# Twelve transposes that nobody reads, beside the chunk scan of a state space layer

## The chip, the cores and the metric

The program runs on one core of a Trainium2 chip. TensorE multiplies matrices and writes PSUM banks; VectorE and ScalarE do elementwise work and empty PSUM; GpSimd does a little elementwise work; DMA queues, most of them issued from SyncE, bring inputs and weights. Each engine works through its own queue in order and waits on semaphores where it needs another engine's result. The metric is the device time of one execution in microseconds (us).

## What is computed

The reference is a trunk of two layers on 512 tokens with 1024 channels. Layer 0 mixes tokens with a diagonal complex state space model, layer 1 with sparse attention (an indexer picks 128 keys for each query); a SwiGLU block follows each. The change concerns layer 0's mixer only:

```python
a_bar = jnp.exp(lam * dt)
b_bar = ((a_bar - 1.0) / lam)[..., None] * lax.complex(b_re, b_im)
bu = jnp.einsum('blgh,gph->blgp', ug, b_bar)              # 64 groups of 16 channels, 64 states each
_, states = lax.associative_scan(_ssm_combine, (a_seq, bu), axis=1)
y = jnp.einsum('blgp,ghp->blgh', states, c).real.reshape(bsz, length, D_MODEL)
y = jax.nn.gelu(y + d_skip * u)
val, gate = jnp.split(y @ w_glu, 2, axis=-1)
return val * jax.nn.sigmoid(gate)
```

## The kernel before

**Tiling.** The 512 tokens are cut into 64 chunks of 8 tokens. The 64 groups are worked in 8 units (u = 0 to 7) of 8 groups. For a unit, `tables(u)` (VectorE) makes the weights W that carry a chunk's tokens into its state; `turned` transposes them on TensorE into a bank of the PSUM tag "tr" and ScalarE copies them out; `chunk_inputs` (TensorE, L679) makes each chunk's contribution S4; `lags` (TensorE, L697, into a "tr" bank that `lags_out` empties on VectorE at L703 as Kd) makes the part within a chunk, which small DMAs spread into M (L706). `turns` and `turns_out` make rotation factors E and ES.

**The scan.** `scan(u)` makes the chunk states X on VectorE: it rotates S4 (L758 to L760, giving z1), runs two real scans over the chunks (L764, giving z), rotates back into a second z1 and z2 (L768, L769) and adds into X (L773). z1, z2 and z lie in scratch buffers 2, 3 and 4, X in 5 or 6. Each scratch buffer is single, so a new tile in it waits until every reader of the old one is done. Buffer 4 also holds the second k3 of `readout` (L791) for every unit but the first; the first k3 uses 5 or 6.

**Outputs.** `readout(u)` makes VV on VectorE (L790 to L792; one buffer). `outputs` (TensorE, L800 from M and L801 from X and VV) writes two accumulators, ScalarE's GELU (L806) makes yg, `out` transposes it (L814, a "tr" bank), and ScalarE and VectorE split it into a high and a low part y (L819, L820). Between these, `filler` puts blocks of the gated projection (three matmuls a step, L272 to L274), for the groups that are ready, into TensorE's queue; ScalarE moves their sums out as `part` (L862). After the eighth unit the rest of the gated projection follows, then the SwiGLU block.

**Order.** The code emits instructions in the order of the loop at L914: scan(u), turns and turned of u+1, tokens of u+2, chunk inputs of u+1, filler, outputs of u, lags of u+1, tables of u+2, readout of u+1, out of u. A planner then fixes each engine's queue before the run, from its own costs and from what is ready by them. Only VectorE and ScalarE, and only up to the end of u = 0, are held to the emitted order among the instructions of that region (L433 to L949). TensorE's queue is the planner's throughout. A tag of PSUM banks has a number of banks, and a new tile waits for one to come free:

```python
    def tr(self):
        return self.pp.tile([P, S], F32, name="tr", bufs=2)
```

Of the kernel before, what the change touches and what calls it, by code (L numbers as in the profile page):

```python
# [20 lines left out]
P = 128  # L21
# [184 lines left out]
class Trunk:  # L206
# [160 lines left out]
    def s5(self, gain_row, x_ap, lre, lim, ldt, b_re, b_im, c_re, c_im, d_ap, w_glu):  # L367
        nc, tc = self.nc, self.tc
        V, PL, AC, PE = nc.vector, nc.gpsimd, nc.scalar, nc.tensor
        ident = self.ident  # L370
# [371 lines left out]
        def turns_out(u, E):  # L742
# [4 lines left out]
            AC.activation(RT[:, u % 2, :, 1:], r8[:, gs].unsqueeze(2).to_broadcast([P, UGP, NCH - 1]), AF.Copy)  # L747
            return ES

        def scan(u, S4, E, ES, between=None):  # L750
            sh = [P, 2, UGP, NCH]
            X = self.scratch(5 + u % 2, [P, UGP, 2, NCH], "X")
            PL.memset(X[:, :, :, 0:1], 0.0)
            z1 = self.scratch(2, sh, "z1")
            z2 = self.scratch(3, sh, "z2")
            z = self.scratch(4, sh, "z")
            Eb = E[:, 0:1].to_broadcast(sh)
            V.tensor_tensor(z1, S4, Eb, op=ALU.mult)  # L758
            V.tensor_tensor(z2, S4[:, ::-1], ES, op=ALU.mult)
            V.tensor_tensor(z1, z1, z2, op=ALU.add)  # L760
            if between is not None:
                between()
            for i in range(2):
                V.tensor_tensor_scan(z[:, i].rearrange("p g c -> p (g c)"), RT[:, u % 2].rearrange("p g c -> p (g c)"),  # L764
                                     z1[:, i].rearrange("p g c -> p (g c)"), 0.0, ALU.mult, ALU.add)
            z1 = self.scratch(2, sh, "z1")
            z2 = self.scratch(3, sh, "z2")
            V.tensor_tensor(z1, z, Eb, op=ALU.mult)  # L768
            V.tensor_tensor(z2, z[:, ::-1], ES[:, ::-1], op=ALU.mult)  # L769
            for i in range(2):  # L770
                for g2 in range(2):
                    hs = slice(g2 * SP, (g2 + 1) * SP)
                    V.tensor_tensor(X[i * SP : (i + 1) * SP, :, g2, 1:], z1[hs, i, :, : NCH - 1],  # L773
                                    z2[hs, i, :, : NCH - 1], op=ALU.add)
            return X
# [52 lines left out]
        groups, n = [], 0  # L828
        while n < len(order):
# [4 lines left out]
            n = m  # L834
# [73 lines left out]
        tokens(1)  # L908
        spread(1)
        X0 = scan(0, S4[0], E[0], ES[0])  # L910
        VV = readout(0)
        W[1] = tables(1)
        normal(2)
        for u in range(UN):  # L914
            more = u + 1 < UN
            X = scan(u, S4[u], E[u], ES[u]) if u else X0
            f = PIECES[u]
            if more:
# [471 lines left out]
```

## Time and profile before

| | |
|---|---|
| time, median of 3 runs | 1292.81 us (1292.65 to 1295.38) |
| the profiled execution's own time | 1294.01 us |
| its span in the profile | 1292.3 us |
| TensorE (PE) busy | 1228.5 us, 95% |
| VectorE (DVE) busy | 769.0 us, 60% |
| ScalarE (ACT) busy | 543.3 us, 42% |
| mean granted TensorE clock | 0.991 |

The profile is of one execution. Times count from the span's start. PE is TensorE's matmuls (a transpose is one of them), PEld its weight loads, DVE is VectorE, ACT ScalarE, POOL GpSimd. A matmul's end is modelled, and consecutive matmuls overlap, so a run of them is shorter than the sum of its members.

### The profile page before, as it was taken

The page shows a single profiled execution, that of the slowest core. Times are in us where ns is not written, and L with a number is a line of the kernel's source. Part 1 is how long each engine was busy: PE and PEld are TensorE (multiplying, and loading weights), DVE is VectorE, ACT ScalarE, POOL GpSimd, SP SyncE. Part 2 cuts the span into 40 slices and gives each one's busy share as a digit, 9 for nine tenths or more (in the row PEclk, how much of TensorE's full clock was granted, in tenths as well). Part 3 has the DMA queues.
Part 4 walks back from the last instruction along what each step waited for, and adds up shares of the span by engine and source line. Part 5 has one row for each costly group of instructions (what it writes and reads, how often), then busy time and mean ns, then how long its engine had stood idle before and what let it go on. Part 6 is the DMA issues. An engine that isn't in the chain of part 4 may idle for free.

```text
span 1292.3 us, 18058 instructions
## 1 busy us (share of the span) xinstructions
PE 1228.5 (95%) x6844; PEld 1052.0 (81%) x6844; DVE 769.0 (60%) x1533; ACT 543.3 (42%) x1225; POOL 152.1 (12%) x180
## 2 busy tenths in 40 slices
PE   5589999999999999999999799999999999999998
PEld 4467778888888888889889799988888888888887
DVE  8999958654444443335899977765754444443221
ACT  5655445433322322322573678864532223332221
POOL 2000000000000000004754444510000000000000
PEclk9989999999999999999999899999999999999999
DMA  5021224333333333332213111111433333333341
GB/s 120 10 78 44 72 86 128 98 98 98 98 98 98 98 90 95 101 98 92 82 34 98 50 50 34 42 34 49 120 101 98 98 98 97 95 93 96 110 116 47
DMA packets 189735, 108.02 MB, mean 84 GB/s; under 512 B 7208, under 2 KB 188560, under 8 KB 189584
## 3 DMA queue, kind: packets, MB, share of 16 engines
q1 hardware_dynamic: 189264, 106.70, 28.4%
q8 instruction: 54, 0.88, 0.3%
q14 instruction: 33, 0.27, 0.1%
q10 hardware_dynamic: 384, 0.16, 0.1%
HBM read 102.39 MB, written 2.10 MB: 81 GB/s over the span
## 4 chain that ended last, share of the span: by engine, by line
PE 74%; DVE 9%; ACT 2%; issue 1%; DMA 1%; POOL 0%; ACTq 0%; DVEq 0%; POOLq 0%
PE acc L272 21%; PE acc L273 21%; PE acc L274 21%; PE acc L1051 5%; PE acc L1256 2%; DVE mask L1159 2%; DVE m L1158 2%; PE tr L1245 1%; DVE mask L1146 1%; PE lg L1229 1%; DVE ro L988 1%; DVE pe L1232 1%; PE lg L1228 1%; DVE kl L1106 0%; PE tr L1088 0%
## 5 line engine op out<-in xcount | busy, mean ns | idle before, releaser
L263 ACT ACTIVATE w_hi<-w_raw 128x1024 fp32r<-128x1024 f32 (+5 forms) x208 | 199.9, 963 | 511.7 <-PE acc L273 464.3
L265 DVE TENSOR_TENSOR w_lo<-w_raw,w_hi 128x1024 fp32r<-128x1024 f32 (+6 forms) x179 | 194.1, 1085 | 142.4 <-ACT w_hi L263 141.1
L272 PE MATMUL acc<-h,w_hi 128*128 128x512 f32 x704 | 274.5, 390 | 0.0
L274 PE MATMUL acc<-h,w_lo 128*128 128x512 f32 x704 | 273.9, 389 | 0.0
L273 PE MATMUL acc<-h,w_hi 128*128 128x512 f32 x704 | 273.7, 389 | 0.0
L1051 PE MATMUL acc<-w_hi,h 128*128 128x256 f32 (+1 forms) x896 | 175.5, 293 | 0.8 <-ACT h L284 0.8
L272 PEld LDWEIGHTS acc<-h,w_hi 128*128 128x128 f32 x704 | 132.1, 188 | 27.9 <-issue 0.5
L273 PEld LDWEIGHTS acc<-h,w_hi 128*128 128x128 f32 x704 | 132.1, 188 | 27.7 <-issue 0.5
L274 PEld LDWEIGHTS acc<-h,w_lo 128*128 128x128 f32 x704 | 132.1, 188 | 27.5
L1051 PEld LDWEIGHTS acc<-w_hi,h 128*128 128x128 f32 x896 | 142.3, 194 | 1.4 <-ACT h L284 1.0
L1051 PE MATMUL acc<-w_lo,h 128*128 128x256 f32 (+1 forms) x448 | 127.2, 289 | 0.3 <-POOL w_lo L267 0.3
L339 DVE TENSOR_TENSOR u<-acc,rinv 128x512 f32<-128x512 f32 x44 | 30.4, 691 | 132.4 <-PE acc L274 132.4
L272 PE MATMUL acc<-f,w_hi 128*128 128x512 f32 x272 | 106.4, 391 | 0.0
L274 PE MATMUL acc<-f,w_lo 128*128 128x512 f32 x272 | 105.9, 389 | 0.0
L273 PE MATMUL acc<-f,w_hi 128*128 128x512 f32 x272 | 105.8, 389 | 0.0
L1051 PEld LDWEIGHTS acc<-w_lo,h 128*128 128x128 f32 x448 | 85.8, 193 | 0.9 <-POOL w_lo L267 0.6
L336 DVE TENSOR_TENSOR g<-acc,rinv 128x512 f32<-128x512 f32 x44 | 30.4, 691 | 85.5 <-PE acc L274 85.4
L267 POOL TENSOR_TENSOR w_lo<-w_raw,w_hi 128x1024 fp32r<-128x1024 f32 (+2 forms) x29 | 69.6, 2412 | 48.1 <-ACT w_hi L263 47.2
L274 PEld LDWEIGHTS acc<-f,w_lo 128*128 128x128 f32 x272 | 51.0, 188 | 10.8
L273 PEld LDWEIGHTS acc<-f,w_hi 128*128 128x128 f32 x272 | 51.1, 188 | 10.5
L272 PEld LDWEIGHTS acc<-f,w_hi 128*128 128x128 f32 x272 | 51.1, 188 | 10.3
L272 PE MATMUL acc<-y,w_hi 128*128 128x512 f32 x128 | 51.1, 405 | 2.8 <-ACT y L819 1.9
(296 smaller groups left out, 1987.0 us busy)
## 6 DMA issues: line engine op xcount, KB each, us to landing
w_raw<-in_ffn_w_gate_up_dram SPq DMA_DIRECT2D x88, 512.0 KB, 3.7
w_raw<-in_ffn_w_down_dram SPq DMA_DIRECT2D x32, 448.0 KB, 3.6
w_raw<-in_dsa_w_in_dram SPq DMA_DIRECT2D x26, 512.0 KB, 3.5
w_raw<-in_ffn_w_down_dram SPq DMA_DIRECT2D x16, 512.0 KB, 3.9
w_raw<-in_dsa_w_o_dram SPq DMA_DIRECT2D x16, 256.0 KB, 2.7
w_raw<-in_s_w_glu_dram SPq DMA_DIRECT2D x6, 384.0 KB, 3.4
xc<-in_x_dram SPq DMA_DIRECT2D x8, 256.0 KB, 5.8
xr<-in_x_dram SPq DMA_DIRECT2D x4, 512.0 KB, 3.5
```

Of the source, the lines that this page charges most:

```text
L263: nc.scalar.activation(hi, raw, AF.Copy)
L265: nc.vector.tensor_tensor(lo, raw, hi, op=ALU.subtract)
L267: lo_engine.tensor_tensor(lo, raw, hi, op=ALU.subtract)
L272: mm(out, lhsT=whi, rhs=xx[:, 0], start=start, stop=False)
L273: mm(out, lhsT=whi, rhs=xx[:, 1], start=False, stop=False)
L274: mm(out, lhsT=wlo, rhs=xx[:, 0], start=False, stop=stop)
L336: nc.vector.tensor_tensor(g, ps[0], rinv, op=ALU.mult)
L339: nc.vector.tensor_tensor(u, ps[1], rinv, op=ALU.mult)
L1051: PE.matmul(pt[:, :n], lhsT=h[k][:, l, ts], rhs=ww, start=(k == 0 and i == 0), stop=(k == KT - 1 and i == 2))
L1158: V.max(m8, sc)
L1159: V.match_replace(out=sc, in_to_replace=m8, in_values=sc, imm_value=GONE)
L1256: PE.matmul(po[s, b][:, i * HD : (i + 1) * HD], lhsT=pT[:, j * P : (j + 1) * P], rhs=vv[j][:, (s * 4 + i) * HD : (s * 4 + i + 1) * HD], st ...
```

## The change

In units 0 to 2, `scan` borrows a "tr" bank twice. After z1 is made, TensorE transposes four 128x128 pieces of it into the first bank; after the two scans it transposes eight pieces of z into the second. Nothing reads either bank. No other instruction is added, removed or edited.

```diff
+        def busy(u, t, n):
+
+            if u < 3:
+                pt = self.tr()
+                for i in range(n):
+                    PE.transpose(pt[:, i % 4 * P : (i % 4 + 1) * P], t[:, i // 2 % 2, i % 2 * 2 : i % 2 * 2 + 2].rearrange("p g c -> p (g c)"), ident)
+
         def scan(u, S4, E, ES, between=None):
...
             V.tensor_tensor(z1, z1, z2, op=ALU.add)
             if between is not None:
                 between()
+            busy(u, z1, 4)
             for i in range(2):
                 V.tensor_tensor_scan(z[:, i].rearrange("p g c -> p (g c)"), RT[:, u % 2].rearrange("p g c -> p (g c)"),
                                      z1[:, i].rearrange("p g c -> p (g c)"), 0.0, ALU.mult, ALU.add)
+            busy(u, z, 8)
             z1 = self.scratch(2, sh, "z1")
             z2 = self.scratch(3, sh, "z2")
```

## Rows read from the trace of the kernel before

**Rows 1.** The page: busy us (share of the span) and instructions of an engine.

```profile
PE 1228.5 (95%) x6844; PEld 1052.0 (81%) x6844; DVE 769.0 (60%) x1533; ACT 543.3 (42%) x1225; POOL 152.1 (12%) x180
```

**Rows 2.** Windows: stretch, busy us of each engine, granted clock, DMA share, GB/s.

```profile
0.00:60.00 60.00, 32.67 (x247) 28.27 (x247) 54.36 (x201) 36.43 (x90) 8.76 (x20) 1.00 0.31 70
61.00:71.00 10.00, 4.70 (x42) 3.75 (x41) 10.00 (x20) 7.97 (x21) 0.11 (x1) 0.50 0.06 12
72.00:103.00 31.00, 26.10 (x228) 21.02 (x228) 30.82 (x59) 15.96 (x34) 0.23 (x2) 1.00 0.27 80
103.00:175.00 72.00, 70.69 (x503) 57.28 (x502) 68.40 (x124) 33.50 (x66) 0.45 (x4) 1.00 0.25 69
175.00:300.00 125.00, 123.81 (x581) 101.82 (x582) 74.73 (x110) 54.87 (x80) 2.21 (x2) 1.00 0.35 103
```

**Rows 3.** The page: chain that ended last, share of the span by engine.

```profile
PE 74%; DVE 9%; ACT 2%; issue 1%; DMA 1%; POOL 0%; ACTq 0%; DVEq 0%; POOLq 0%
```

**Rows 4.** The same chain in order of time, its first pieces: start, us, what.

```profile
175.14 0.04 issue
175.18 0.50 PE acc L273
```

**Rows 5.** Waits of VectorE up to 103 us: total us, times, longest.

```profile
DVE ldb L450 <- DMA ldt<-in_s_log_dt_dram: 2.2, 1, 2.2
DVE ones L220 <- PEq L1376: 0.9, 1, 0.9
DVE prm L456 <- PE lg L454: 0.4, 1, 0.4
```

**Rows 6.** Windows of one microsecond around the change of the granted clock.

```profile
61.00:62.00 1.00, 0.50 (x6) 0.31 (x3) 1.00 (x3) 0.95 (x5) 0.00 (x0) 0.50 0.00 0
...
71.00:72.00 1.00, 1.00 (x19) 0.93 (x16) 1.00 (x3) 0.36 (x1) 0.00 (x0) 0.91 0.36 86
```

**Rows 7.** Timeline: start, us, engine line operation out<-in; four transposes of W.

```profile
29.44 1.09 PE L668 MATMUL tr<-ident,W 128*128 128x128 f32 x4 [0.36 <-DVE W L660]
...
52.57 0.66 PE L668 MATMUL tr<-ident,W 128*128 128x128 f32 x4
```

**Rows 8.** Timeline, unit 0; in brackets the engine's idle time before and its releaser.

```profile
40.84 0.69 DVE L760 TENSOR_TENSOR z<-z,z 128x512 f32<-128x512 f32 x1
41.63 1.27 DVE L764 TENSOR_TENSOR_SCAN z<-RT,z 128x256 f32<-128x256 f32 x2
42.94 0.69 DVE L768 TENSOR_TENSOR z<-z,E 128x512 f32<-128x512 f32 x1
...
45.66 1.09 PE L800 MATMUL acc<-M,U 128*64 128x128 f32 x4 [9.27 <-DMA M<-Kd]
```

**Rows 9.** Timeline, unit 1.

```profile
66.45 0.28 DVE L703 TENSOR_TENSOR Kd<-tr,Dd 128x128 f32<-128x128 f32 x1
...
66.79 2.12 PE L668 MATMUL tr<-ident,W 128*128 128x128 f32 x8 [5.30 <-DVE Kd L703]
...
69.11 0.70 DVE L760 TENSOR_TENSOR z<-z,z 128x512 f32<-128x512 f32 x1
...
70.92 1.28 DVE L764 TENSOR_TENSOR_SCAN z<-RT,z 128x256 f32<-128x256 f32 x2
...
75.90 0.40 PE L801 MATMUL acc<-VV,X 128*64 128x128 f32 x2 [0.94 <-DVE X L773]
...
76.23 0.69 DVE L791 TENSOR_TENSOR k<-Csw,psti 128x512 f32<-128x512 f32 x1
...
78.76 0.38 PE L801 MATMUL acc<-VV,X 128*64 128x128 f32 x2
...
81.05 1.28 DVE L790 TENSOR_TENSOR VV<-Cst,hC 128x512 f32<-128x512 f32 x2
```

**Rows 10.** Timeline, unit 2.

```profile
86.63 1.86 PE L697 MATMUL tr<-Cz,W 128*128 128x32 f32 x16
...
89.31 0.27 DVE L703 TENSOR_TENSOR Kd<-tr,Dd 128x128 f32<-128x128 f32 x1
...
91.29 0.50 PE L272 MATMUL acc<-y,w_hi 128*128 128x512 f32 x1 [0.86 <-ACT part L862]
...
93.86 0.40 PE L801 MATMUL acc<-VV,X 128*64 128x128 f32 x2 [0.91 <-DVE X L773]
```

## The prediction

> **What bounds the kernel now.** I read the page first, for who is busy overall, then the windows by stretch, because one average hides several stages. TensorE is busy 95% of the span and VectorE 60% [rows 1], but by stretch it splits [rows 2]. Up to 60 us TensorE works little more than half the time and VectorE 54.36 of 60. From 61 to 71 us VectorE works every microsecond and TensorE 4.70 of 10. From 72 to 103 us VectorE idles 31.00 - 30.82 = 0.2 us, TensorE 31.00 - 26.10 = 4.9 us. From 103 us on TensorE idles 72.00 - 70.69 = 1.3 us out of 72, and it stays full beyond 175 us. So the state space layer has two halves: VectorE's queue sets the pace until about 100 us, TensorE's work sets it after that. The chain of waits agrees as far as it reaches: TensorE holds 74% of the span and VectorE 9% [rows 3]. But followed in order of time its first piece lies at 175 us [rows 4], so for the units that the change touches I must read queues instead.
>
> The view of waits lists what VectorE waited for up to 103 us: loads and start-up at the very beginning, and TensorE only once there, 0.4 us for the first parameters [rows 5]. In units 0 to 2 it never waits for TensorE. This is the pivot: a faster TensorE there cannot make VectorE's queue shorter.
>
> The clock is read in two ways. The granted column is 0.50 from 61 us, after TensorE had stood idle, and is back during the microsecond after 71 [rows 6]. Four 128x128 transposes take 1.09 us at 29.44, but 0.66 us at 52.57 [rows 7]; within the stretch at 0.50 eight take 2.12 us, as slow as the early ones [rows 9]. So the column's 1.00 in the first 60 us [rows 2] is not to be believed throughout: by the durations TensorE ran at the lower of its two levels (1.2 GHz) early on, and at the upper one (2.4 GHz) at 52 us and again from some time after 71 us.
>
> **The change, part by part.** It removes nothing and moves nothing in the source. It adds 3 x (4 + 8) = 36 transposes of 128x128, two borrowings of one of the two "tr" banks per unit, and, unseen in the text, readers: z1 and z sit in single buffers, so what VectorE next writes there must wait until TensorE has read.
>
> *Price of one.* At the lower level four cost 1.09 us, so 0.27 each; at the upper level four cost 0.66 with the tail of the last [rows 7], and I take 0.15 each in a run of several.
>
> *Unit 0.* z1 is complete at 40.84 + 0.69 = 41.53, z at 41.63 + 1.27 = 42.90 [rows 8]. TensorE has nothing to do in the 9.27 us up to 45.66, where it waits for the DMA of M [rows 8]. Twelve at the lower level are 12 x 0.27 = 3.3 us, done by about 45.1. The cover is that DMA; without it 3.3 us. VectorE's next write to z1, L768, starts at 42.94; four transposes from 41.6 end at 42.7. Cost 0, with 0.2 us to spare.
>
> *Unit 1.* z1 is complete at 69.81, z at 72.20 [rows 9]. The idle stretch of TensorE, 5.30 us up to 66.79, is over by then: it waits for Kd, which frees a tr bank, and Kd stands ahead of L760 in VectorE's queue [rows 9]. So the transposes can't stand where the clock falls; they land in the busy run 66.79 to 74.96, ahead of the outputs' L801, which waits 0.94 us for X [rows 9]. Added: four at the lower level (before 71.1), 1.09 us, and eight at the upper, 1.2 us, together 2.3. Less the 0.94 of idle, TensorE comes to L801 about 1.35 us late, at 77.3. Who waits for that? VectorE's L790 at 81.05 needs the readers of VV gone, which ended near 78.76 + 0.38 = 79.14 [rows 9]: 1.9 us of room, enough.
>
> *Unit 2.* Twelve at the upper level cost 12 x 0.15 = 1.8 us. Up to this unit's L801 TensorE has waits of 0.86 us (for ScalarE's part) and 0.91 us (for X) [rows 10]. Lateness 1.35 + 1.8 = 3.15; less both waits 1.4, less only the second 2.2. Kd at 89.31 has its input from 86.63 + 1.86 = 88.49 on [rows 10]; with TensorE 1.95 late by then, VectorE stalls some 1.1 us, but in parallel with TensorE's own lateness, so the larger counts and not the sum.
>
> *Afterwards.* Behind 103 us TensorE is the pace and its remaining 1.3 us of idle time [rows 2] could swallow up to that much. So the end moves by 2.2 at most and 1.4 - 1.3 = 0.1 at least. I take 1.4, because those later waits mostly follow TensorE's own results and shift with it. Units 3 to 7 get no new instruction.
>
> *The clock.* Whether transposes would lift it, no row separates: the rise at 71 us follows twelve transposes and then the matmuls of L679. If the stretch from 61 to 71 ran at the upper level, its 4.70 busy microseconds would be 2.35 and the saving would just pay unit 1's 2.3; unit 2's 1.8 fits its two waits of 1.77: sum 0 instead of +1.4. It can't be below 0 by this path, because L801 waits for X from VectorE anyway.
>
> The Trainium skill, "TensorE: Matmul & The Clock Gate", section Part 4: PE-mode transpose, speaks against such a lift: a transpose does not count as TensorE activity in the way a matmul does. By that rule the sum stays +1.4 and the case with 0 drops out; no row here shows a stretch of transposes alone, so the trace neither agrees nor disagrees.
>
> *Sum.* The profiled execution took 1294.01 us (span 1292.3 and 1.7 around it), so 1295.4; that execution lies 1.2 above the median of the runs, 1292.81, so as a median 1294.2. About 0.2% (2.6 us) is what a measurement of this kernel can tell from no change, the three runs themselves spreading from 1292.65 to 1295.38.
>
> **The rivals.**
>
> *Slower: VectorE waits for the reader.* TensorE executes in the planner's order, so the place of the transposes in its queue decides. After L769 the buffer of z is next written by unit 2's second k3, L791, at 76.23 [rows 9]. If the eight stand ahead of L801, they are read by about 76 to 77 and VectorE loses at most 1. If they stand behind the outputs (which end near 79.14, or 80.5 with the lateness), they are read at 81.7, and VectorE's queue stands still for 5.5 us: Kd, W, the next z1 and X behind it all slip, and nothing in 0.2 us of idle time takes it back. In unit 0 the like: z1's four behind L800 would hold L768 from 42.94 until about 47.9, 4.9 us. Price about +5, median 1297.8. The point from which it decides: TensorE must reach unit 1's eight by 75.0. For it: two banks only, and pk and the next tiles contend for them. Against it: in both units z1 and z are ready before what else waits (M lands at 45.66, X at 75.90), so an order by readiness puts the transposes first.
>
> *Faster: the planner reorders.* The two extra borrowings of a bank can change who gets the bank that Kd holds until 66.73. If unit 2's L668 no longer waited those 5.30 us, TensorE could bring forward blocks of the gated projection into its 4.9 us of idle time between 72 and 103 us; less unit 2's 1.8 that is -3.1, median 1289.7. For it: the whole 5.30 us wait is a wait for a bank. Against it: the order is fixed before the run, and the blocks need y's low half and w_lo from VectorE's full queue.
>
> *The clock stays up* (above): 1292.8, no change.
>
> **How the numbers follow.** My forecast, lateness of TensorE partly absorbed, 0.42; the clock case 0.08; VectorE waiting 0.28; reordered faster 0.22. Faster 0.22, same 0.42 + 0.08 = 0.50, slower 0.28. The likeliest case's own range is 1292.9 to 1295.0 (the 0.1 and 2.2 of its bounds). The other two mechanisms hold half the chance, so the range reaches to both of their prices: down to 1289.5, and up to 1298.5, a little above 1297.8 because stalls in two units can add.
>
> **What the changed profile would show.** Unit 0's twelve between 41.5 and 45.2 at some 0.27 us each and L768 still at 42.9; TensorE's idle stretch before L668 and the granted 0.50 after it still there; unit 1's L801 one to two microseconds late with its wait for X gone; VectorE's idle time between 40 and 103 us under a microsecond more. I am wrong if L768 or L791 show a wait for TensorE of several microseconds, if the stretch 61 to 71 us reads 1.00, or if the instructions of VectorE's queue stand in another order.

## The result

The changed kernel takes 1302.56 us (median of 6 runs, 1302.04 to 1303.66) against 1293.42 us before (6 runs, 1292.65 to 1295.38): a ratio of 1.0069, 95% interval 1.0056 to 1.0082, so 8.9 us slower (7.2 to 10.6). The prediction was 1294.2 us, no measurable change, with a range of 1289.5 to 1298.5.

The page after shows more TensorE work, as it must, and no more work for VectorE:

```profile
span 1300.9 us, 18136 instructions
...
PE 1233.0 (95%) x6880; PEld 1059.1 (81%) x6880; DVE 767.4 (59%) x1533; ACT 543.7 (42%) x1225; POOL 152.0 (12%) x180
```

The windows after, of the stretches of [rows 2]:

```profile
0.00:60.00 60.00, 31.52 (x201) 27.42 (x202) 47.97 (x189) 31.07 (x75) 8.75 (x20) 1.00 0.31 70
61.00:71.00 10.00, 4.90 (x60) 4.30 (x60) 8.97 (x20) 9.84 (x29) 0.00 (x0) 0.73 0.01 2
72.00:103.00 31.00, 21.90 (x168) 18.34 (x168) 30.82 (x60) 10.81 (x23) 0.11 (x1) 0.72 0.23 66
103.00:175.00 72.00, 70.71 (x570) 59.58 (x569) 68.40 (x123) 40.19 (x80) 0.45 (x4) 1.00 0.22 61
```

VectorE did 47.97 us of work by 60 us where it had done 54.36 [rows 2]: 6.4 us less. Most of the loss lies ahead of 60 us. The view of VectorE's waits up to 103 us, which held nothing of TensorE's behind the start before [rows 5], names the place:

```profile
DVE z L777 <- PE tr L755: 6.5, 1, 6.5
...
DVE z L766 <- ACT ES L746: 0.6, 1, 0.6
...
DVE z L765 <- PE lg L679: 0.3, 1, 0.3
DVE k L800 <- PE acc L810: 0.2, 1, 0.2
```

(Lines behind L747 moved by 7 to 9 with the added code: L768 is now L777, L773 is L782, L791 is L800, L800 and L801 are L809 and L810. L755 is the new transpose.) The timeline after shows VectorE in unit 0, to be held against [rows 8]: the same starts up to the scan, then a hole.

```profile
40.84 0.69 DVE L767 TENSOR_TENSOR z<-z,z 128x512 f32<-128x512 f32 x1
41.63 1.27 DVE L772 TENSOR_TENSOR_SCAN z<-RT,z 128x256 f32<-128x256 f32 x2
49.39 0.69 DVE L777 TENSOR_TENSOR z<-z,E 128x512 f32<-128x512 f32 x1 [6.49 <-PE tr L755]
...
82.05 1.72 DVE L782 TENSOR_TENSOR X<-z,z 64x252 f32<-64x252 f32 x4
...
100.59 1.71 DVE L782 TENSOR_TENSOR X<-z,z 64x252 f32<-64x252 f32 x4
```

L777 overwrites z1's buffer, and the four transposes that read z1 had not run. The chain of waits after, in order of time, says why not. Unlike before [rows 4] it now reaches back into this stretch:

```profile
43.36 2.67 DMA M<-Kd
46.02 0.35 issue
46.37 1.08 PE acc L809 x4
47.46 1.05 PE tr L609 x4
48.50 0.87 PE tr L755 x4
49.37 0.02 issue
49.39 0.69 DVE z L777
```

TensorE stood idle: at the head of its queue were the first output matmuls L809, which waited for the DMA of M. Behind them came the token transposes L609, and only then the transposes of z1, complete since 41.5. Before, unit 1's and unit 2's X were made at these times:

```profile
74.49 1.72 DVE L773 TENSOR_TENSOR X<-z,z 64x252 f32<-64x252 f32 x4
...
92.45 1.71 DVE L773 TENSOR_TENSOR X<-z,z 64x252 f32<-64x252 f32 x4
```

So unit 1's X is 82.05 - 74.49 = 7.56 us late. The waits add up to that: L777 starts 49.39 - 42.94 = 6.45 later, and 0.6 + 0.3 + 0.2 = 1.1 of smaller waits follow. In between VectorE runs the same instructions, from 59 us on partly in another order. Unit 2's X is 8.14 late, the span 1300.9 - 1292.3 = 8.6 longer; the view of waits up to 103 us has nothing for those last 0.6 us.

### The profile page after: what moved, and what is told of

Read it like the earlier page. It is cut to its first block, busy times and chain, and to the rows that moved or that the text cites. A ratio compares the mean times of both kernels' runs of the same rounds, so it can differ in the third digit from the quotient of the medians.

```text
span 1300.9 us, 18136 instructions
## 1 busy us (share of the span) xinstructions
PE 1233.0 (95%) x6880; PEld 1059.1 (81%) x6880; DVE 767.4 (59%) x1533; ACT 543.7 (42%) x1225; POOL 152.0 (12%) x180
## 4 chain that ended last, share of the span: by engine, by line
PE 84%; DVE 10%; ACT 3%; issue 1%; DMA 1%; POOL 0%; ACTq 0%; SPq 0%; DVEq 0%; POOLq 0%
PE acc L272 22%; PE acc L273 22%; PE acc L274 22%; PE acc L1060 10%; PE acc L1265 2%; PE tr L1254 1%; PE acc L809 1%; PE acc L810 1%; PE tr L1097 1%; PE tr L697 1%; PE lg L1238 1%; DVE pe L1241 1%; PE lg L1237 0%; DVE mask L1168 0%; DVE kl L1115 0%
```

## The experiments

Each ran beside the kernel before; a ratio is to that kernel, with its 95% interval, and a loss in us is the ratio less 1, times the median before. Unless said otherwise an edit is to the changed kernel.

**Unit 0 alone.**

```diff
-            if u < 3:
+            if u < 1:
```

> The change in unit 0 alone. Theory A (VectorE's rewrite of z1, L777, waits 6.5 us because TensorE reads z1 only behind the outputs' first matmuls, which wait for the DMA of M, and behind the token transposes): nearly all of the loss is here, 1299 to 1301 us, and L777 again shows a wait for TensorE of about 6.5 us. Theory B (the loss comes from units 1 and 2, where unit u+1's transposes of W stand behind those of z): no loss here, 1293 to 1295. Theory C (TensorE's added work and the clock that falls once more): a third of the loss, about 1296.

Measured: 1301.9 us, ratio 1.0058 (1.0041 to 1.0075), so +7.5 us of the 8.9. A little above theory A's figure, but far from B's and C's. VectorE's waits, then its timeline:

```profile
DVE z L777 <- PE tr L755: 6.4, 1, 6.4
```

```profile
49.31 0.69 DVE L777 TENSOR_TENSOR z<-z,E 128x512 f32<-128x512 f32 x1 [6.40 <-PE tr L755]
```

**Units 1 and 2 alone.**

```diff
-            if u < 3:
+            if 0 < u < 3:
```

> The change in units 1 and 2 without unit 0. Theory A: 1294.5 to 1297, no wait of VectorE above 1 us before 103 us. Theory B: 1300 to 1303, the loss stays whole. Theory C: two thirds of it, about 1299.

Measured: 1295.27 us, ratio 1.0014 (1.0005 to 1.0024), +1.8 us. The two parts, 7.5 and 1.8, make the whole of 8.9 within their intervals. VectorE has no wait beyond those of [rows 5]. TensorE, however, does not do here what I had drawn:

```profile
69.92 1.09 PE L755 MATMUL tr<-ident,z 128*128 128x128 f32 x4 [8.42 <-DVE z L767]
71.73 0.66 PE L755 MATMUL tr<-ident,z 128*128 128x128 f32 x2 [0.72 <-DVE z L772]
72.18 1.06 PE L668 MATMUL tr<-ident,W 128*128 128x128 f32 x4
```

W's transposes, at 66.79 before [rows 9], now start at 72.18, behind z1's and two of z's, although unit 2's W was complete at 60.3 (L660 at 59.59) and Kd had freed a bank at 66.7: the idle stretch got longer (8.42 us), not filled. TensorE still comes to its outputs only 1.8 us late (L810 at 77.66, L801 at 75.90 before [rows 9]), since the stretch had slack.

**A buffer of its own for the second z1.** TensorE's transposes all stay; only VectorE need no longer wait for them. (a3 is free until unit 3's y.)

```diff
-            z1 = self.scratch(2, sh, "z1")
+            z1 = self.slot("a3", sh, "z1own") if u < 3 else self.scratch(2, sh, "z1")
```

> All 36 transposes in the same banks, but the second z1 of units 0 to 2 goes to a buffer of its own, so that VectorE need not wait until TensorE has read the first. Theory A: L777 starts near 43 us again, unit 0's outputs come about 3 us later because twelve slow transposes stand ahead of them, the sum 1295 to 1298. Theories B and C: no change against the changed kernel, 1301 to 1303, since TensorE's queue and its work stay.

Measured: 1295.13 us, ratio 1.0010 (1.0001 to 1.0020). TensorE's timeline and then VectorE's:

```profile
45.71 1.08 PE L809 MATMUL acc<-M,U 128*64 128x128 f32 x4 [8.44 <-DMA M<-Kd]
46.72 1.11 PE L609 MATMUL tr<-ident,xn 128*128 128x128 f32 x4
47.63 1.06 PE L755 MATMUL tr<-ident,z 128*128 128x128 f32 x4
```

```profile
42.81 0.69 DVE L777 TENSOR_TENSOR z1own<-z,E 128x512 f32<-128x512 f32 x1
```

The transposes stand as late as in the changed kernel, and no engine waits for them. They do not stand ahead of the outputs, as the expectation had it, and L809 starts where L800 did before (45.66 [rows 8]). So the loss is VectorE's wait for the reader; neither TensorE's work nor its order costs 7 us.

**The token transposes emitted behind unit 0's scan.** No instruction of VectorE or ScalarE changes its place in the emitted order.

```diff
         normal(1)
-        tokens(1)
-        spread(1)
         X0 = scan(0, S4[0], E[0], ES[0])
+        tokens(1)
+        spread(1)
```

> All 36 transposes, z1 in its one buffer, but the code emits the token transposes of unit 1 (and the spread after them) behind unit 0's scan instead of ahead of it; VectorE's and ScalarE's emitted orders stay. Theory A with its cause (tr banks are handed out in emission order, so the bank for z1 comes only after the one for the tokens): TensorE's order has z1's and z's transposes ahead of the outputs, L777 starts near 43 us, and the time is that of units 1 and 2 alone, 1294.5 to 1297. If the bank order is not the cause, z1's transposes stay behind and the time stays at 1301 to 1303.

Measured: 1296.34 us, ratio 1.0016 (1.0006 to 1.0025), +2.1 us, about what units 1 and 2 cost alone. TensorE's timeline, then VectorE's:

```profile
41.67 2.83 PE L755 MATMUL tr<-ident,z 128*128 128x128 f32 x12 [4.96 <-DVE z L767]
46.63 0.62 PE L809 MATMUL acc<-M,U 128*64 128x128 f32 x4 [2.13 <-DMA M<-Kd]
```

```profile
43.01 0.69 DVE L777 TENSOR_TENSOR z<-z,E 128x512 f32<-128x512 f32 x1
```

This is what the prediction had drawn for unit 0. One call's place in the code decides it: a bank of the tag is asked for in emission order, the tokens' request stood first, and their input xn comes from ScalarE only at 45.3 (L600 from 44.02 in the changed kernel), 3.8 us behind z1.

The same for unit 0's twelve without the others (both edits together):

> Unit 0's twelve alone, with the tokens' bank asked for behind them. Theory A: as the kernel before, 1293 to 1295, because the wait of L777 was the whole loss of unit 0. If unit 0's twelve cost anything beside that wait: 1296 or more.

Measured: 1294.45 us, ratio 1.0003 (0.9993 to 1.0012). With the order mended, unit 0's twelve cost nothing that can be told.

**Only z's eight, and only z1's four.**

```diff
-            busy(u, z1, 4)
```

> The change without the four transposes of z1: only z's eight, units 0 to 2. Theory A (it is the read of z1 that holds VectorE in unit 0; z's buffer is written again only by unit 1's second k3): L777 starts near 43 us, 1294.5 to 1297. If any transposes in this place cost the same: 1301 to 1303.

Measured: 1294.8 us, ratio 1.0011 (1.0002 to 1.0020).

```diff
-            busy(u, z, 8)
```

> The change without z's eight transposes: only z1's four, units 0 to 2. Theory A: unit 0's wait of L777 stays whole (6 to 6.5 us), since it ends with the fourth transpose, and units 1 and 2 lose less: 1299 to 1301.5. If the number of transposes counts: a third of the loss, 1296 to 1297.

Measured: 1301.24 us, ratio 1.0063 (1.0048 to 1.0078). A third of the transposes make nearly the whole loss; the other two thirds make 1.4 us. VectorE's waits with z1's four alone (one line of code less, so L777 is L776 here):

```profile
DVE z L776 <- PE tr L755: 6.6, 1, 6.6
```

**The same number of transposes, of the identity.** They read nothing that VectorE writes.

```diff
-                    PE.transpose(pt[...], t[...].rearrange("p g c -> p (g c)"), ident)
+                    PE.transpose(pt[...], ident, ident)
```

> All 36 transposes in the same banks, but of the identity instead of z1 and z, so that nothing that VectorE writes is read. Theory A: L777 starts near 43 us; TensorE still does all the work: 1293.5 to 1296. Theory C (the work itself): 1301 to 1303.

Measured: 1293.71 us, ratio 0.9999 (0.9990 to 1.0009). TensorE's added work, 36 transposes, and the added borrowing of banks cost nothing that can be told. L777 starts at 42.98. The identity is ready from 3 us on, and yet its first four transposes stand behind the tokens' in unit 0, as z1's did:

```profile
46.90 1.11 PE L609 MATMUL tr<-ident,xn 128*128 128x128 f32 x4
47.81 1.06 PE L755 MATMUL tr<-ident 128*128 128x128 f32 x4
```

So it is not their input that keeps them there.

**Banks of another tag.**

```diff
-                pt = self.tr()
+                pt = self.lg()
```

> All 36 transposes, reading z1 and z as in the change, but into banks of the tag lg instead of tr. Theory A with its cause (the order in which tr banks are handed out puts z1's transposes behind the tokens' in unit 0, and ahead of the next unit's W in units 1 and 2): L777 starts near 43 us and W's transposes no longer stand behind z's, so 1293 to 1295.5. If reading z1 and z costs by itself: 1296 or more.

Measured: 1295.23 us, ratio 1.0008 (0.9999 to 1.0017). The emitted order is the changed kernel's, and in unit 0 the transposes now run as soon as z1 is there:

```profile
41.59 2.92 PE L755 MATMUL lg<-ident,z 128*128 128x128 f32 x12 [4.83 <-DVE z L767]
```

L777 starts at 43.02, and unit 2's W is transposed at 66.60, as before (66.79). Whether the last 1 us is real stays open.

**What a higher clock is worth**, tried in the kernel before (no transposes of z1 or z). First 30 in its idle time of unit 0, then 14 in its idle time behind unit 0's out:

```diff
+        pt = self.lg()
+        for _ in range(30):
+            PE.transpose(pt[:, :P], ident, ident)
         X0 = scan(0, S4[0], E[0], ES[0])
```

> The kernel before with 30 transposes of the identity in an lg bank ahead of unit 0's scan, where TensorE is idle for 9 us: does a stretch of transposes alone lift the clock? If it does, they get shorter within the run, from 0.27 to about 0.15 us each, and unit 0's outputs run at the upper level from their start; the time stays at 1292.5 to 1294.5 all the same, since VectorE never waits for TensorE there. If it does not, all 30 take 0.27 us, 8 us together, and the time is as before too. If a warm TensorE is worth something at the end, 1290 to 1292.

Measured: 1293.73 us, ratio 0.9996 (0.9987 to 1.0006). The 30 took 4.80 us, where at 0.27 each they would have taken 8.1, so the clock rose among them; but TensorE then idled and met the outputs at the lower level again:

```profile
36.23 4.80 PE L912 MATMUL lg<-ident 128*128 128x128 f32 x30
45.67 0.98 PE L800 MATMUL acc<-M,U 128*64 128x128 f32 x4 [4.65 <-DMA M<-Kd]
```

```diff
             out(u, yg)
+            if u == 0:
+                pt = self.lg()
+                for i in range(14):
+                    PE.transpose(pt[:, i % 4 * P : (i % 4 + 1) * P], y[0][:, 0, i % 4 * P : (i % 4 + 1) * P].bitcast(F32), ident)
```

> The kernel before with 14 transposes of unit 0's finished y, read by nobody, in an lg bank behind unit 0's out: they stand in TensorE's idle stretch between 62 and 67 us, where the clock falls. The question is what a clock kept up or brought back sooner is worth. Theory A (VectorE's queue sets the pace there): the granted clock is back by 68 or 69 us instead of 71, and the time is 1293 to 1294.5, no change. If a TensorE at the upper level is worth something: 1290 to 1292. If the transposes delay unit 2's W: 1295 to 1296.

Measured: 1294.49 us, ratio 1.0006 (0.9993 to 1.0019). The clock came back one to two microseconds sooner than before [rows 6], later than the 68 or 69 us expected, as windows of one microsecond show:

```profile
68.00:69.00 1.00, 1.00 (x7) 0.74 (x5) 1.00 (x2) 0.03 (x1) 0.00 (x0) 0.50 0.03 6
69.00:70.00 1.00, 1.00 (x7) 0.82 (x7) 1.00 (x2) 0.80 (x2) 0.00 (x0) 0.76 0.09 19
70.00:71.00 1.00, 1.00 (x29) 0.83 (x29) 1.00 (x3) 0.99 (x3) 0.00 (x0) 1.00 0.24 52
```

But it fell again where it had stayed up before: the granted clock is 0.50 from 77 to 79 us, and the first two matmuls L801 took 0.66 us where they had taken 0.40 [rows 9]:

```profile
76.83 0.66 PE L801 MATMUL acc<-VV,X 128*64 128x128 f32 x2 [0.93 <-DVE X L773]
```

So neither run had a TensorE that was faster through the stretch, and what that would be worth is not measured. Both profiles have a wait of VectorE that the kernel before has not, 1.1 and 1.0 us of L791 for unit 0's outputs L801; in the second it comes ahead of the added transposes, so it is not their doing.

No variant was faster than the kernel before by more than its interval.

## Why the prediction was wrong

**The reading of the bound was right.** VectorE's queue sets the pace up to 100 us: with unit 0 alone, a wait of 6.4 us in it came out at the end as 7.5, while 36 more transposes on TensorE that VectorE did not wait for cost nothing that can be told. That a faster TensorE is worth nothing there follows from VectorE's waits before [rows 5]; it is not shown by a run, since the two runs on the clock did not keep it up.

**The step that failed is unit 0's "Cost 0, with 0.2 us to spare"**, and behind it the sentence against the slower rival: that z1 and z "are ready before what else waits", so that "an order by readiness puts the transposes first". Readiness by data did not decide: z1's four were ready at 41.5 and started at 48.30, and so late that L777 lost 6.45 us. A transpose also needs its tr bank, and the order in which those are asked for is the emitted one, in which unit 1's tokens came ahead. Moving that one call (tokens emitted behind the scan) turns the loss of unit 0 off with every transpose still there, and so does another tag of banks; transposes of the identity, ready long before, stand as late as z1's. The emitted order was there to read in the code, and TensorE's timeline before uses the tr tiles in it (unit 2's W at 66.79, tokens at 68.71, lags at 71.44, unit 1's out at 79.82), though that sequence alone would fit readiness too. I read the tag only as "two banks" and asked whether one was free, not who was next in line for it.

**The rival itself was right in kind and named the instruction.** It said that z1's four behind the outputs' matmuls would hold L768 from 42.94 to about 47.9, 4.9 us. It was 49.39, 6.45 us: the outputs' matmuls, which wait for M's DMA, started 0.7 later than before (46.37 against 45.66), and the tokens' transposes stood in front too, about 1.1 more by the chain. It got 0.28 of the chance and the range ended at 1298.5, which holds its price of 5 us but not 7.5. The mechanism's other place, z's buffer at unit 2's second k3 (L791, now L800), did not decide: z's eight alone cost 1.4 us.

**Units 1 and 2** were forecast at +1.4 and cost 1.8 (0.6 to 3.1), but not by the steps given, so that the two figures lie close is luck. I let the transposes fall into TensorE's busy run; they came first and pushed W's transposes 5.4 us back. The wait for a bank in that place was read rightly, but not that z1's request came ahead of W's. That this order is what costs there is likely, since the identity's transposes cost nothing, but the intervals of 1.0014, 1.0008 and 0.9999 lie too close together to show it.

**"The clock stays up" and the faster rival** did not come. The granted clock fell in the changed kernel too and once more in unit 2's stretch: 0.72 on the mean from 72 to 103 us, where it had been 1.00 [rows 2]. No run contradicts the statement that by this path the sum can't be below 0. Of the signs of being wrong, the wait of L768 came, and VectorE's queue stood in another order from 59 us on; the stretch from 61 to 71 us read 0.73, not 1.00.

## What to carry to other kernels

An instruction that nobody reads from is still a reader: it holds the buffer that it reads until its own queue lets it run. Before adding one, look for who next overwrites its input, and for everything that stands ahead of it in its queue, including who is ahead in line for its output bank; where the overwriting engine sets the pace, the wait is paid in full, here 6.4 us as 7.5. Filling idle time to keep a clock up makes sense only on the engine that sets the pace in that stretch; this is argued from the waits, as neither run here kept the clock up.

## What the runs showed of the hardware

Transposes alone bring TensorE's clock up. In the run with the identity TensorE did only transposes after 5.20 us of idle time, twelve of its own and eight of W:

```profile
66.74 2.97 PE L755 MATMUL tr<-ident 128*128 128x128 f32 x12 [5.20 <-DVE Kd L703]
69.50 1.78 PE L668 MATMUL tr<-ident,W 128*128 128x128 f32 x8
71.31 0.66 PE L609 MATMUL tr<-ident,xn 128*128 128x128 f32 x4
```

Windows of one microsecond show the granted clock, in the third column from the right:

```profile
70.00:71.00 1.00, 1.00 (x7) 1.00 (x5) 1.00 (x3) 0.34 (x1) 0.00 (x0) 0.50 0.22 51
71.00:72.00 1.00, 0.97 (x8) 0.54 (x9) 1.00 (x2) 0.85 (x2) 0.00 (x0) 0.99 0.39 95
```

It rose from 0.50 (1.2 GHz) at about 71 us, and the next four took 0.66 us instead of 1.07 to 1.09. With the 14 transposes behind unit 0's out it rose between 69 and 70 us, likewise after nothing but transposes. The sentence of the Trainium skill that the prediction cites ("TensorE: Matmul & The Clock Gate", Part 4: PE-mode transpose), by which a transpose does not count as a matmul does, would have kept the clock at 0.50 here. The trace does not agree for these fp32 transposes, and the measurement decides; whether the transpose mode that the section speaks of was on in them, the trace does not show.
